# A hybrid encoder layer on one core: other blocks for two first product units, a norm's matmul six blocks later, plain passes in four groups

## The chip, the cores and the metric

The kernel runs on one core of one Trainium2 chip. The metric is device microseconds of the whole program. The engines are named as in the profile: PE (TensorE, matmuls), PEld (its weight loads), DVE (VectorE), ACT (ScalarE), POOL (GpSimd) and SP (SyncE, which here only issues DMAs).

## The reference

One encoder layer for 512 tokens of width 2048, in float32:

```python
h = rms_norm(x, norm_gains[l, 0])
# h @ w_in -> 11 blocks of 512 columns, shared by four mixers:
# stick-breaking attention, differential attention, a gated linear recurrence, a short gated conv
mixed = jnp.concatenate([y_sb, y_df, y_lru, y_sc], axis=-1) @ w_out[l]
x = x + rms_norm(mixed, norm_gains[l, 1])
h = rms_norm(x, norm_gains[l, 2])
u = causal_dwconv(h @ w_up, conv_w)          # 2048 -> 8192, conv of 3 taps
g, up = jnp.split(u, 2, axis=-1)
x = x + rms_norm((gelu(g) * up) @ w_down, norm_gains[l, 3])   # 4096 -> 2048
```

The change lies in the second half: the norm before the feed-forward part, the up projection and the down projection.

## The kernel before, in words

Activations are kept transposed, features on the 128 partitions and tokens along the free axis. Every float32 operand is split into a high part `hi` (rounded to the type that PE multiplies in) and a low part `lo` (the rest). A product is the sum of three passes: weight hi by activation hi, weight hi by activation lo, weight lo by activation hi. Splitting is a copy on ACT (`w_hi`, L99 and L1048; `a`, L189) and a subtraction on DVE (`w_lo`, L100 and L1049; L190).

**Groups.** `group` (from L125) makes four output blocks of 128 features from 8 chunks of weights. A chunk is 512 KB, loaded by SP into one of three `w_raw` buffers, then split into one of three `w_hi` and three `w_lo` buffers. With `both`, the tokens of one half (256) have their hi and lo side by side in memory, and the two passes with weight hi are joined into one matmul of 512 columns (hi into the left half of a PSUM bank, lo into the right), followed by one of 256 columns for weight lo. The two halves of the bank then have to be added: `sum_of` copies the left half on ACT (L952) and adds the right on DVE (L953). Without `both` all three passes have 256 columns and go into one place, and a copy suffices.

**Order of the work.** PE runs its instructions in the order in which the program is written. Work beside the matmuls is hung on a clock of blocks: `tick` counts four blocks a chunk, and `at(block, fn)` runs `fn` when the clock gets there. The other engines' instructions are put in order ahead of time by a scheduler that goes by priorities: what stands under `high_priority` (weight loads and splits, taking results out of PSUM) goes first. Each engine, and each DMA queue, then runs its list strictly in that order.

**The second norm.** The out projection's last two column groups are done for the first 256 tokens, then for the last 256. After each of the two halves `residual` (L842) normalises, adds x, and hangs the squares of the new x (L868 on ACT, summed by L870 on DVE), the scaled copies (L876) and `norm2` on the clock. `norm2` (L880) sums the squares over partitions with a matmul by ones on PE (L885), works out the reciprocal root (L200 to L206) and makes the operands of the up projection (L891, L189, L190). After the second half `sums_of_h` (L904) also makes the sums of operands T1, T3 and T4 (L911 to L918).

**Plain up units.** `up_plain` (L1002) does the first four of 32 blocks of gate and of value as four ordinary groups: gate and value for the first tokens, then gate and value for the last.

**Product units.** The rest of the up projection, and most of the down projection, run as `seven` (L1063): a 2 by 2 block product with seven products in place of eight. A unit loads the four weight blocks a11, a12, a21, a22 and makes the sums s1 = a21 + a22, s2 = a11 + s1, s3 = a11 + a21 and s4 = a12 + s2, each sum by a DVE add (L1054) or by an accumulating DMA from POOL's queue (L1058, from s3's own copy of a11). The products come in the order 11 (a11), 21 (a12), T2 (s2), T1 (s1), T3 (s3), 22 (s4), T4 (a22); L1079 are its passes with weight hi, L1084 those with weight lo. T2 and T3 go into the PSUM bank that 11 used, so each must wait until `take` has read it (ACT L1143, DVE L1144 to L1146 in the up units, DVE L1247 in the down units).

Blocks of weights lie in `w_raw` buffers or in `spare`, a tile that takes over the place of an operand that is done with: in the up units the second `mg` tile (free after the splits of `split_t2` and of T4, L190), in the down units `act`'s tile `a0` (free when PE has read the last plain down group). The first unit of each kind (`first`) finds these places still in use. `ystage` and `gst` are two small pools of 512 KB buffers (`ys`), through which the down projection's operands are loaded.

Of the kernel before, what the change touches and what calls it, by code (L numbers as in the profile page):

```python
# [9 lines left out]
F32 = mybir.dt.float32  # L10
# [38 lines left out]
def trunk(ctx: ExitStack, tc: tile.TileContext, xT, params, consts, wgate, w_in, w_out, w_up0, w_up, w_dn, w_dns, out):  # L49
# [734 lines left out]
    with ExitStack() as ph:  # L784
# [57 lines left out]
        def residual(hf):  # L842

            ts = HALVES[hf]
            ss1[hf].rstd(rstd1[:, ts])
            acc = ph2.tile([P, 2, S // 2], F32, name="s2")
            for q in range(4):
                for i in range(2):
                    m = mg[q][hf][:, 2 * i:2 * i + 2]
                    V.tensor_tensor(out=m, in0=m, in1=repeated(rstd1[:, ts], 2), op=ALU.mult)  # L850
                if q < 2:
                    G.dma_start(out=xs[q][hf], in_=mg[q][hf], accum_op=ALU.add)
            for q in range(2, 4):
                for i in range(2):
                    m, x = (t[q][hf][:, 2 * i:2 * i + 2] for t in (mg, xs))
                    V.tensor_tensor(out=x, in0=x, in1=m, op=ALU.add)
            for n, q in enumerate((0, 2, 1, 3)):
                at(clock[0] + 19 + 4 * n // 3, lambda n=n, q=q: squares(hf, q, acc, n == 0))
                at(clock[0] + 25 + 2 * n, lambda q=q: scaled(hf, q))
            at(clock[0] + 37, lambda: norm2(hf, acc))  # L860

        def squares(hf, q, acc, first):

# [138 lines left out]
        def up_plain(half, ts):  # L1002
            def evac(u, ps):
                if ts.start == 0:
                    ub[half, u] = up_tile()
                t = ub[half, u]
                sum_of(t[:, 2 + ts.start:2 + ts.stop], ps)
                return (lambda: done(u)) if ts.stop == S else None

            def done(u):  # L1010
                if half == 0:
                    gates[u] = conv(ub[half, u], half, u)
                else:
                    later.append(lambda: glu(u, gates[u], conv(ub[half, u], half, u)))
            group([w_up0[half, c] for c in range(8)], act_h, act_l, natural, evac,
                  mm_tile if half == 0 else pa_tile, ts, both=act_b)

        for half in range(2):
            up_plain(half, H0)
# [17 lines left out]
        def by4(t):  # L1037
            return flat(t).rearrange("p (a b) -> p a b", a=4)
# [24 lines left out]
        def seven(src, tops, take, first=False, place=None):  # L1063
# [23 lines left out]
            if place is None:  # L1087
                a11, a21 = raw(spare[n], src[0, 0]), raw(spare[2 + n], src[1, 0])
                a12, s3, a22 = (w_raw() for _ in range(3))
            else:  # L1090
                a11, a12, a21 = (w_raw() for _ in range(3))
                s3, a22 = place
                raw(a11, src[0, 0])
                raw(a21, src[1, 0])
            if first:
                raw(a22, src[1, 1])
                if place is None:
                    add(s3, a11, a21)
                add(a21, a21, a22)
            else:  # L1100
                dma_add(a21, by4(src[1, 1]))
            if place is not None or not first:
                raw(s3, src[0, 0])
                dma_add(s3, by4(src[1, 0]))
            s1 = a21
            raw(a12, src[0, 1])
            o11 = operand(a11)
            add(a11, a11, s1)
            s2 = a11
# [26 lines left out]
        def up_unit(unit):  # L1136
# [9 lines left out]
                    taken.append(V.tensor_tensor(out=t, in0=t, in1=ps[:, 256:512], op=ALU.add))  # L1146

            taken = []
            steps = seven(w_up[unit - 4], tops, take, first=unit == 4)
            next(steps)  # L1150
            gate = conv(u[0], 0, unit)
            if later:
# [88 lines left out]
        def down_unit(n):  # L1241
# [4 lines left out]
                    for part in (ps[:, 0:256], ps[:, 256:512]):  # L1246
                        V.tensor_tensor(out=t, in0=t, in1=part, op=ALU.subtract if i else ALU.add)  # L1247

            place = (spare[0], by4(gst.tile([P, 2, S], F32, name="ys"))) if n == 0 else None
            for _ in seven(w_dns[n], dtops, take, n == 0, place):  # L1250
                pass

# [168 lines left out]
```

## Time and profile before

| | |
|---|---|
| runs of the kernel before | 1786.59, 1786.46 and 1779.22 us, median 1786.46 |
| the profiled execution | 1781.3 us, of which its span is 1779.6 |
| PE busy | 1728.9 us, 97% of the span |
| PE weight loads busy | 1472.4 us, 83% |
| DVE busy | 1259.5 us, 71% |
| ACT busy | 903.0 us, 51% |
| POOL busy | 161.1 us, 9% |

Busy is the union of an engine's instructions. The ends of matmuls are modelled, so the pace of PE is read from the starts of matmuls that follow each other and not from their durations.

### The profile page before, as it was taken

Reading aid. Unit: us, or ns where it says so; the run is one execution under the profiler, and the core shown is the slowest. Engines: PE = TensorE matmul, PEld = TensorE weight load, DVE = VectorE, ACT = ScalarE, POOL = GpSimd, SP = SyncE. Lnnn points to the kernel's source line nnn. Section 1 sums busy time; section 2 is a strip of 40 time slices with the busy share of each in tenths; the row PEclk is TensorE's granted clock in tenths of the full one; section 3 lists DMA queues with packets and bytes.
Section 4 is the critical chain, followed back from the end, with each engine's and each line's share of the span. In section 5 each row is a group of like instructions: output and inputs, shape, how many; then the busy total and the mean of one; then the engine's idle time right before and its main releaser. Section 6 shows DMA issues by size and latency. Waiting matters only on the chain. (4 is left out here: it accounts for less than half of the span.)

```text
span 1779.6 us, 23837 instructions
## 1 busy us (share of the span) xinstructions
PE 1728.9 (97%) x8896; PEld 1472.4 (83%) x8896; DVE 1259.5 (71%) x1943; ACT 903.0 (51%) x1351; POOL 161.1 (9%) x228
## 2 busy tenths in 40 slices
PE   8999999999999999999999999999999999999995
PEld 7778788887888888788788888888888878888884
DVE  7885576566656424889898888788888886775337
ACT  6443576665334335776555555555555663333342
POOL 0000011100000011100011111111111001110120
PEclk9999999999999999999999999999999999999998
DMA  7234222242222625775788888888888668878233
GB/s 254 81 103 144 83 78 78 77 154 80 92 95 89 201 96 188 224 237 166 206 225 244 238 227 223 235 232 218 239 229 229 194 195 215 224 196 287 95 114 135
DMA packets 97020, 308.06 MB, mean 173 GB/s; under 512 B 10468, under 2 KB 14820, under 8 KB 96904
## 3 DMA queue, kind: packets, MB, share of 16 engines
q1 hardware_dynamic: 80056, 247.29, 41.2%
q0 software_dynamic: 15696, 57.15, 17.1%
q10 hardware_dynamic: 1152, 2.10, 0.3%
q8 instruction: 70, 1.15, 0.3%
q14 instruction: 46, 0.38, 0.1%
HBM read 265.59 MB, written 21.24 MB: 161 GB/s over the span
## 5 line engine op out<-in xcount | busy, mean ns | idle before, releaser
L100 DVE TENSOR_TENSOR w_lo<-w_raw,w_hi 128x1024 fp32r<-128x1024 f32 (+1 forms) x207 | 253.2, 1224 | 248.1 <-PE mm L157 140.4
L99 ACT CAST w_hi<-w_raw 128x1024 fp32r<-128x1024 f32 (+1 forms) x207 | 216.4, 1045 | 307.2 <-PE mm L157 192.0
L157 PE MATMUL mm<-a,w_hi 128*128 128x512 f32 x1280 | 310.1, 392 | 2.1 <-DVE t L330 2.1
L1079 PE MATMUL mm<-a,w_hi 128*128 128x512 f32 x1088 | 275.9, 396 | 8.4 <-DVE m L1247 5.3
L157 PEld LDWEIGHTS mm<-a,w_hi 128*128 128x128 f32 x1280 | 238.7, 188 | 52.4 <-DVE t L330 2.6
L1048 ACT CAST w_hi<-w_raw 128x1024 fp32r<-128x1024 f32 x145 | 152.0, 1049 | 202.1 <-PE mm L1079 164.5
L1079 PEld LDWEIGHTS mm<-a,w_hi 128*128 128x128 f32 x1088 | 197.6, 191 | 44.9 <-issue 5.7
L1049 DVE TENSOR_TENSOR w_lo<-w_raw,w_hi 128x1024 fp32r<-128x1024 f32 x145 | 177.0, 1221 | 37.6 <-ACT w_hi L1048 37.4
L157 PE MATMUL mm<-a,w_lo 128*128 128x512 f32 x640 | 166.2, 397 | 0.0
L1084 PEld LDWEIGHTS mm<-a,w_lo 128*128 128x128 f32 x1088 | 148.6, 191 | 12.0 <-DVE w_lo L1049 1.3
L1084 PE MATMUL mm<-a,w_lo 128*128 128x256 f32 x1088 | 151.8, 282 | 0.9 <-DVE w_lo L1049 0.9
L1079 PE MATMUL mm<-xs,w_hi 128*128 128x512 f32 x576 | 144.3, 392 | 0.2 <-DVE ub L1146 0.2
L157 PEld LDWEIGHTS mm<-a,w_lo 128*128 128x128 f32 x640 | 117.8, 189 | 24.1 <-issue 1.5
L1048 ACT CAST w_hi<-mg 128x1024 fp32r<-128x1024 f32 x84 | 87.6, 1044 | 81.1 <-PE mm L1079 81.1
L1079 PEld LDWEIGHTS mm<-xs,w_hi 128*128 128x128 f32 x576 | 103.7, 189 | 18.9 <-DVE ub L1146 0.4
L1049 DVE TENSOR_TENSOR w_lo<-mg,w_hi 128x1024 fp32r<-128x1024 f32 x84 | 102.4, 1220 | 19.9 <-ACT w_hi L1048 19.9
L1079 PE MATMUL mm<-mg,w_hi 128*128 128x512 f32 x352 | 88.3, 393 | 1.4 <-DVE m L1247 1.4
L1084 PEld LDWEIGHTS mm<-xs,w_lo 128*128 128x128 f32 x576 | 78.6, 190 | 5.6
L1146 DVE TENSOR_TENSOR ub<-ub,mm 128x256 f32<-128x256 f32 x196 | 81.2, 414 | 0.0
L1084 PE MATMUL mm<-xs,w_lo 128*128 128x256 f32 x576 | 80.3, 282 | 0.0
L1079 PEld LDWEIGHTS mm<-mg,w_hi 128*128 128x128 f32 x352 | 63.3, 189 | 13.0 <-ACT xs L189 1.6
L1247 DVE TENSOR_TENSOR m<-m,mm 128x256 f32<-128x256 f32 x112 | 46.5, 416 | 36.5 <-PE mm L1084 36.3
(308 smaller groups left out, 2725.1 us busy)
## 6 DMA issues: line engine op xcount, KB each, us to landing
w_raw<-in_w_up_dram SPq DMA_DIRECT2D x115, 512.0 KB, 5.7
w_raw<-in_w_in_dram SPq DMA_DIRECT2D x87, 512.0 KB, 3.3
mg<-in_w_up_dram SPq DMA_DIRECT2D x56, 512.0 KB, 4.2
w_raw<-in_w_out_dram SPq DMA_DIRECT2D x48, 512.0 KB, 3.3
w_raw<-in_w_dn_dram SPq DMA_DIRECT2D x38, 512.0 KB, 3.3
w_raw<-mg POOLq DMA_DIRECT2D x28, 512.0 KB, 6.2
mg<-in_w_up_dram POOLq DMA_DIRECT2D x27, 512.0 KB, 7.8
w_raw<-in_w_up_dram POOLq DMA_DIRECT2D x27, 512.0 KB, 8.8
```

The lines of the kernel that those rows point to most:

```text
L99: w_split.append(A.copy(out=hi[:, sl], in_=raw[:, sl]))
L100: V.tensor_tensor(out=lo[:, sl], in0=raw[:, sl], in1=hi[:, sl].bitcast(F32), op=ALU.subtract)
L157: T.matmul(pss[u], lhsT=a, rhs=b, start=c == 0 and kk == 0 and not low and i == 0, stop=False)
L1048: w_split.append(A.copy(out=by4(hi), in_=v))
L1049: V.tensor_tensor(out=by4(lo), in0=v, in1=by4(hi).bitcast(F32), op=ALU.subtract)
L1079: T.matmul(ps.rearrange("p (a t) -> p a t", a=2), lhsT=hi[:, k * P:(k + 1) * P], rhs=tops[name][k], start=first and k == 0, stop=False, **kw)
L1084: T.matmul(ps[:, 0:256], lhsT=lo[:, k * P:(k + 1) * P], rhs=tops[name][k][:, 0], start=False, stop=k == 7, **kw)
L1146: taken.append(V.tensor_tensor(out=t, in0=t, in1=ps[:, 256:512], op=ALU.add))
L1247: V.tensor_tensor(out=t, in0=t, in1=part, op=ALU.subtract if i else ALU.add)
```

## The change

Three edits stand in one diff.

```diff
-            at(clock[0] + 37, lambda: norm2(hf, acc))
+            at(clock[0] + 43, lambda: norm2(hf, acc))
...
-                sum_of(t[:, 2 + ts.start:2 + ts.stop], ps)
+                A.copy(out=t[:, 2 + ts.start:2 + ts.stop], in_=ps)
...
             group([w_up0[half, c] for c in range(8)], act_h, act_l, natural, evac,
-                  mm_tile if half == 0 else pa_tile, ts, both=act_b)
+                  mm_tile if half == 0 else pa_tile, ts)
...
                 a11, a12, a21 = (w_raw() for _ in range(3))
                 s3, a22 = place
                 raw(a11, src[0, 0])
+                raw(a12, src[0, 1])
                 raw(a21, src[1, 0])
             if first:
                 raw(a22, src[1, 1])
-                if place is None:
-                    add(s3, a11, a21)
                 add(a21, a21, a22)
             else:
                 dma_add(a21, by4(src[1, 1]))
-            if place is not None or not first:
-                raw(s3, src[0, 0])
-                dma_add(s3, by4(src[1, 0]))
+            raw(s3, src[0, 0])
+            dma_add(s3, by4(src[1, 0]))
             s1 = a21
-            raw(a12, src[0, 1])
+            if place is None:
+                raw(a12, src[0, 1])
...
-            steps = seven(w_up[unit - 4], tops, take, first=unit == 4)
+            place = (spare[0], spare[2]) if unit == 4 else None
+            steps = seven(w_up[unit - 4], tops, take, unit == 4, place)
...
-            place = (spare[0], by4(gst.tile([P, 2, S], F32, name="ys"))) if n == 0 else None
+            place = [by4(t.tile([P, 2, S], F32, name="ys")) for t in (ystage, gst)] if n == 0 else None
```

The second norm's matmul moves by six blocks on the clock, a chunk and a half. On PE, at the first of its two places (the out projection's last group, `pa<-a`, two rows for one chunk and two of its operands), it moves behind the passes with weight lo of one chunk and all passes of the next:

```order
 L149 MATMUL pa<-a_82,w_lo 128x256 x8
 L149 MATMUL pa<-a_80,w_hi 128x512 x8
-L885 MATMUL mm<-s_5766,con 128x256 x2
 L149 MATMUL pa<-a_80,w_lo 128x256 x8
 L149 MATMUL pa<-a_80,w_hi 128x512 x8
 L149 MATMUL pa<-a_80,w_lo 128x256 x8
+L885 MATMUL mm<-s_5766,con 128x256 x2
 L149 MATMUL pa<-a_81,w_hi 128x512 x8
```

Between the old and the new place now stand 24 matmuls.

The first up unit (unit 4) takes a11, a12 and a21 into `w_raw` buffers and leaves s3 and a22 to the shared place `mg`. SP's queue before, from the last chunk of the plain up units (L98) on; `w_raw_7168` is a22, the four `mg` are a11 and a21 of units 4 and 5, `w_raw_7166` is a12:

```order
L98 DMA w_raw_7122<-in_w_up0_dram 128x1024
L1042 DMA w_raw_7168<-in_w_up_dram 128x1024
L1042 DMA mg_7156<-in_w_up_dram 128x1024 x4
L1042 DMA w_raw_7166<-in_w_up_dram 128x1024
L1042 DMA mg_7156<-in_w_up_dram 128x1024
```

And of the change; `w_raw_7404`, `7405` and `7406` are a11, a12 and a21, the first two `mg` are s3's copy of a11 and a22, the next two are unit 5's a11 and a21:

```order
L98 DMA w_raw_7358<-in_w_up0_dram 128x1024
L1042 DMA w_raw_7404<-in_w_up_dram 128x1024
L1042 DMA w_raw_7405<-in_w_up_dram 128x1024
L1042 DMA mg_7396<-in_w_up_dram 128x1024 x2
L1042 DMA w_raw_7406<-in_w_up_dram 128x1024
L1042 DMA mg_7396<-in_w_up_dram 128x1024 x2
```

The blocks of the first two products now stand ahead of every load that needs the shared place; a21 still stands behind two of them.

The first down unit takes s3 into `ystage` where it had the shared place `a0`. DVE before, from the last split of the down projection's operands (L190) on; the row with `a0` is the split of s3, L1247 are the takes:

```order
L190 TENSOR_TENSOR mg_12363<-ys_12520,mg_12363 128x512
L1247 TENSOR_TENSOR m30_12342<-m30_12342,mm_12735 128x256
L1049 TENSOR_TENSOR w_lo_12799<-w_raw_12740,w_hi_12798 128x1024
L1247 TENSOR_TENSOR m30_12342<-m30_12342,mm_12735 128x256
L1247 TENSOR_TENSOR m30_12342<-m30_12342,mm_12737 128x256 x2
L1049 TENSOR_TENSOR w_lo_12821<-a0_12733,w_hi_12820 128x1024
L1247 TENSOR_TENSOR m30_12342<-m30_12342,mm_12735 128x256
L1049 TENSOR_TENSOR w_lo_12843<-w_raw_12739,w_hi_12842 128x1024
L1247 TENSOR_TENSOR m30_12342<-m30_12342,mm_12735 128x256
```

And of the change; s3 is `ys_12975`:

```order
L190 TENSOR_TENSOR mg_12604<-ys_12761,mg_12604 128x512
L1247 TENSOR_TENSOR m30_12583<-m30_12583,mm_12977 128x256
L1049 TENSOR_TENSOR w_lo_13041<-w_raw_12982,w_hi_13040 128x1024
L1247 TENSOR_TENSOR m30_12583<-m30_12583,mm_12977 128x256
L1247 TENSOR_TENSOR m30_12583<-m30_12583,mm_12979 128x256
L1049 TENSOR_TENSOR w_lo_13063<-ys_12975,w_hi_13062 128x1024
L1247 TENSOR_TENSOR m30_12583<-m30_12583,mm_12979 128x256
L1247 TENSOR_TENSOR m30_12583<-m30_12583,mm_12977 128x256
```

The order on DVE is nearly the same; what differs is the place from which s3 is read.

## Rows read from the trace of the kernel before

**Rows 1.** The page's first part: engine, busy us, share of the span, instructions.

```profile
PE 1728.9 (97%) x8896; PEld 1472.4 (83%) x8896; DVE 1259.5 (71%) x1943; ACT 903.0 (51%) x1351; POOL 161.1 (9%) x228
```

**Rows 2.** Who waited for whom, PE: us in total, times, longest.

```profile
PE mm L885 <- DVE s L870: 7.5, 2, 4.0
```

**Rows 3.** Stretches: length, busy us of each engine, granted clock, DMA share.

```profile
740.00:750.00 10.00, 6.01 (x21) 4.84 (x21) 6.40 (x9) 7.67 (x16) 0.00 (x0) 0.66 0.51 165
...
744.00:863.00 119.00, 114.25 (x621) 99.64 (x622) 106.73 (x142) 83.03 (x132) 1.76 (x2) 0.95 0.59 195
...
804.50:857.60 53.10, 53.10 (x305) 46.68 (x304) 52.03 (x60) 37.05 (x47) 0.00 (x0) 1.00 0.51 168
```

**Rows 4.** Timeline of PE, first norm matmul: start, us, engine, line [idle before <-releaser].

```profile
738.32 2.11 PE L149 MATMUL pa<-a,w_hi 128*128 128x512 f32 x8
744.42 2.04 PE L885 MATMUL mm<-s,con 128*128 128x256 f32 x4 [3.98 <-DVE s L870]
745.90 2.27 PE L149 MATMUL pa<-a,w_lo 128*128 128x256 f32 x8
...
750.39 0.88 PE L149 MATMUL pa<-a,w_lo 128*128 128x256 f32 x6
```

**Rows 5.** Timeline of DVE at the same place.

```profile
740.19 3.48 DVE L100 TENSOR_TENSOR w_lo<-w_raw,w_hi 128x1024 fp32r<-128x1024 f32 x3
743.60 0.68 DVE L870 TENSOR_TENSOR s<-s,f 128x512 f32<-128x512 f32 x1
```

**Rows 6.** Timeline of PE, second norm matmul.

```profile
792.66 2.00 PE L149 MATMUL pa<-a,w_hi 128*128 128x512 f32 x8
798.15 2.04 PE L885 MATMUL mm<-s,con 128*128 128x256 f32 x4 [3.49 <-DVE s L870]
...
804.54 1.10 PE L149 MATMUL pa<-a,w_lo 128*128 128x256 f32 x8
```

**Rows 7.** Timeline of PE inside the first plain up group.

```profile
770.29 2.00 PE L149 MATMUL mm<-a,w_hi 128*128 128x512 f32 x8
772.13 1.12 PE L149 MATMUL mm<-a,w_lo 128*128 128x256 f32 x8
773.09 2.00 PE L149 MATMUL mm<-a,w_hi 128*128 128x512 f32 x8
```

**Rows 8.** Groups of DVE instructions, 750 to 862: shapes, count | busy, mean ns | idle.

```profile
L953 DVE TENSOR_TENSOR ub<-ub,mm 128x256 f32<-128x256 f32 x8 | 3.2, 416 | 0.4 <-ACT ub L952 0.4
```

**Rows 9.** Timeline of PE, start of the first up unit.

```profile
862.41 2.11 PE L1079 MATMUL mm<-a,w_hi 128*128 128x512 f32 x8 [0.83 <-ACT w_hi L1048]
...
868.81 3.62 PE L1079 MATMUL mm<-a,w_hi 128*128 128x512 f32 x8 [2.18 <-ACT w_hi L1048]
872.26 0.99 PE L1084 MATMUL mm<-a,w_lo 128*128 128x256 f32 x7
```

**Rows 10.** Timeline of all engines ahead of it (SPq is SP's queue).

```profile
855.27 2.35 DVE L190 TENSOR_TENSOR mg<-mg 128x1024 fp32r<-128x1024 f32 x2
...
857.65 1.75 SPq L1042 DMA_DIRECT2D mg<-in_w_up_dram  x4
...
859.44 0.75 SPq L1042 DMA_DIRECT2D w_raw<-in_w_up_dram  x1
```

**Rows 11.** Timeline of PE, first down unit.

```profile
1467.40 2.06 PE L1079 MATMUL mm<-a,w_hi 128*128 128x512 f32 x8 [2.38 <-DVE m L1247]
...
1472.09 1.11 PE L1084 MATMUL mm<-a,w_lo 128*128 128x256 f32 x8
1476.17 3.65 PE L1079 MATMUL mm<-a,w_hi 128*128 128x512 f32 x8 [2.96 <-DVE m L1247]
1479.64 1.14 PE L1084 MATMUL mm<-a,w_lo 128*128 128x256 f32 x8
```

**Rows 12.** Timeline of DVE in the first down unit.

```profile
1457.82 1.22 DVE L1054 TENSOR_TENSOR w_raw<-w_raw,ys 128x1024 f32<-128x1024 f32 x1 [1.06 <-DMA ys<-in_w_dns_dram]
...
1473.00 1.22 DVE L1049 TENSOR_TENSOR w_lo<-a,w_hi 128x1024 fp32r<-128x1024 f32 x1 [4.77 <-ACT w_hi L1048]
```

## Prediction

> **What bounds the kernel now.** I read the engines' shares first: PE is busy 97% of the span, DVE 71% [rows 1]. So PE is the engine whose idle time counts, and the question is where in the second half it waits. The view of who waited for whom has the norm matmul (L885) first: 7.5 us in two waits for the summed squares [rows 2]. The timelines then give each place, and the stretches tell what the clock does after a wait.
>
> Four places matter. At each I take as lost the time between what the matmuls would have needed at full pace and when the next ones started. That pace is read where PE is fed: eight matmuls of 512 columns start over 1.84 us (0.230 each), eight of 256 over 0.96 (0.120 each) [rows 7].
>
> *First norm matmul.* Eight wide matmuls start at 738.32 and would be done by 740.16. L885 starts at 744.42, waiting for DVE's last sum [rows 4]. The granted clock over 740 to 750 is 0.66, so half of full pace (1.2 of 2.4 GHz) for a part of it [rows 3]: L885's four matmuls take 1.48 us until 745.90, I count 0.74 at full pace. Then 0.96 and 1.84 should lead to 743.70; the next narrow pass starts at 750.39 [rows 4]. Lost: 6.7 us.
>
> *Second norm matmul.* In the same way 792.66 + 1.84 + 0.74 + 2.80 = 798.04, against 804.54 [rows 6]. Lost: 6.5.
>
> *First up unit.* 0.83 before the first pass; from 862.41 on, two wide passes and a narrow one need 4.64 us, which leads to 867.05, and the next narrow one starts at 872.26 [rows 9]. Lost: 5.2 + 0.8 = 6.0. The cause stands in the queue: SP holds its four loads into `mg` until DVE's split ends at 857.6, and the load of a12, needed for the second product, stands behind them (859.44) [rows 10].
>
> *First down unit.* A wait of 2.38 ahead of T2 and one of 2.96 ahead of T3 [rows 11]. The second is a queue on DVE: the split of s3 waits 4.77 us for its cast, which waits for s3 itself, and the takes that free the bank for T3 stand behind it [rows 12]. From 1472.09 a narrow pass and a wide one should end at 1474.89; the next narrow pass starts at 1479.64 [rows 11]. Lost: 4.75.
>
> **The change, part by part.**
>
> *The norm's matmul, six blocks later.* A chunk and a half of matmuls that needs nothing from the norm comes ahead of it: 0.96 + 1.84 + 0.96 = 3.76 us at the first place (in the second, plain group 0.96 + 1.92 + 0.96). At the first place these need w_lo, and the first of DVE's three splits ends at about 741.4 (740.19 and a third of 3.48, rounded up) [rows 5], so PE waits 1.2 us there; the norm comes at 740.16 + 1.2 + 3.76 = 745.1, after the last sum (743.60 + 0.68 = 744.3) [rows 5]. Gain 6.7 − 1.2 = 5.5. At the second place PE gets to the norm at 794.50 + 3.84 = 798.3, in the old times; before, the sum released it at 798.15 [rows 6]. No wait, gain 6.5. What is late next: the operands for the next group, which are made from the norm. The chain from rstd to them lies on DVE, beside four chunks of matmuls (4 × 2.80 = 11.2 us) where it had five and a half; at 98% DVE busy (52.03 of 53.10) in the stretch behind the second norm [rows 3] this is the thinnest cover in the change. I price it at 0.3 us for each half and keep 3 us each as the other end.
>
> *Plain passes.* For 64 pairs of operand and chunk in each of four groups, 0.230 + 0.120 becomes 3 × 0.120 [rows 7]: 0.010 × 256 = 2.6 us more on PE, all on the path. DVE loses 16 adds of 0.416 [rows 8], 6.7 us in a stretch where it is nearly full, which is what the splits need if PE is to run without its stalls. Stretches of 24 narrow matmuls do not occur before; those of eight keep 0.120 to their end, and I take that.
>
> The Trainium skill ("TensorE: Matmul & The Clock Gate", section Back-to-back issue gap) gives N/2.4 + 2.5 ns for a matmul alone at full clock, 109 and 216 ns; by it three narrow passes would cost 2.5 ns more than the joined pair, 0.6 us in all (an estimate from that page), and it adds that in a stream of weight loads and matmuls both set the pace. This case's rows have 120 and 230, so the trace is above the formula, and the rows decide.
>
> *First up unit.* a11 and a12 no longer wait for `mg`: both come with the buffers that the last plain chunks free. s3 and a22 go to `mg`, and a21 has to come behind them in SP's queue. With these in place T2 is the next that can be late: it needs a21 + a22, added to a11, cast. `mg` comes free when DVE has made the splits of T4 and T2. Counted in the order of the change, DVE has between the second norm and that 16 splits of weights and 16 steps of the operands of the same size (1.16 each, the pitch of the three [rows 5]) and 16 of half the size: 46 us, and it starts on them some 2.5 us after PE has passed the norm. PE has 20 plain chunks of 2.88 = 57.6 until the unit. So `mg` should be free 7 to 9 us ahead of the unit, where it was 4.8 ahead (857.6 to 862.4) [rows 9, 10]. The queue's five loads took until the a12 cast that released PE at 868.81, 9 us from its issue [rows 9, 10]; a21 now is the third. I forecast 0.5 us left of 6.0, gain 5.5; the ends are 0 and 6.0.
>
> *First down unit.* s3's load no longer waits for PE to be done with `a0`; in SP's new order it even stands ahead of a22's, which arrives at 1457.8 [rows 12]. Before, s3's load and its accumulating DMA were both done between there and the split at 1473.00 [rows 12], 15 us; now only the second is left after 1457.8, and it has until about 1471 for T3 to start on time. So DVE's list should no longer stop there: gain 4.75. The wait of 2.38 ahead of T2 comes from DVE's row of work behind a22's arrival, which the order leaves as it was: it stays.
>
> **Sum.** −5.5 − 6.5 + 0.6 + 2.6 − 5.5 − 4.75 = −19.0 us. The profiled execution took 1781.3, so 1762.3 for one like it. The median of the runs shown is 5.2 above that execution, the lowest run 2.1 below: I forecast **1764**.
>
> **Rivals.**
>
> *DVE takes it back.* DVE had 12.3 us idle between 744 and 863 (106.73 busy of 119) [rows 3], while PE stalled. If it keeps as much idle time and only loses the 6.7 us of adds, PE meets late splits or a late s2 in unit 4. Then the two norms, the plain passes and unit 4 together give at most 6.7 us; with the down unit 11.5, so 1770 against the profiled execution and 1772 on the forecast's scale. For it: 98% [rows 3]. Against it: in that stretch of 53 us PE had no wait, so a full DVE kept up with PE at full pace while it still had the adds to do.
>
> *The place does not help unit 4.* a21 is behind two loads that wait for `mg`, so if `mg` is not free sooner the wait moves from the second product to the third, and only the two norms and the down unit give: −13.5, 1768 against the profiled execution and near 1770 on the forecast's scale. For it: the new queue order. Against it: the earlier split order on DVE.
>
> *Narrow passes hold PE up.* The other side. If in a run of 24 the pace falls from 0.120 to what a weight load takes from start to end (PEld busy 1472.4 over 8896 is 0.166 each [rows 1]), 768 matmuls cost 35 us more: +16, 1797 as measured against the profiled execution. It decides from 0.145 on (19 us over 768) and is slower by over 0.5% from 0.157. Against it: eight in a row show no such drift [rows 7].
>
> **Chances.** Forecast, with 15 us or more gained: 0.62. DVE takes it back: 0.20, of which half are gains above 0.5% (8.9 us, about what a measurement of this kernel can tell from no change). Unit 4 not helped: 0.11, still faster. Narrow passes slow: 0.04. Something else that leaves no change: 0.03. So faster 0.83, same 0.13, slower 0.04. The range: down to 1756, where the down unit's T2 wait goes too, nothing new is left over, and the runs are as low as the lowest of before; up to 1775, where DVE's rival and the median's 5 us come together.
>
> **What would show it.** Right: L885 with no wait for L870 and the clock at 1.00 behind it; a plain chunk of 24 matmuls in 2.88 us; unit 4's first three passes at full pace; T3 in the first down unit without a wait, T2 still with one of about 2.4. Wrong: waits of PE for L190's operands at the start of a plain up group, for a weight's w_lo (L100) in them, or ahead of T2 in unit 4; starts of narrow matmuls further apart than 0.120.

## The result and the profile after

The changed kernel took 1772.14 us (median of 6 runs, 1768.99 to 1775.05) against 1786.53 for the kernel before (median of 6). The ratio is 0.9937, 95% interval 0.9922 to 0.9953: faster by 8 to 14 us. A second set of runs gave 0.9928 (0.9914 to 0.9942). The forecast was 1764. The medians shown differ by more than this ratio says (14.4 us, a ratio of 0.992); how the two fit together is open. The direction was right and the time lies in the range, but the 15 us or more to which the forecast gave 0.62 did not come.

The profiled execution took 1772.23 us, 9.1 less than that of before (1781.3), so what follows has to add up to 9.1, where the forecast's sum is 19.0. PE's busy share hardly moves; its busy time counts the plain passes and the slow stretches too. The first part of the page:

```profile
PE 1727.5 (98%) x9152; PEld 1484.7 (84%) x9152; DVE 1252.2 (71%) x1926; ACT 902.1 (51%) x1351; POOL 162.0 (9%) x229
```

The view of who waited for whom, PE from 737 to 920 (us in total, times, longest). The wait of L885 that led in [rows 2] is gone. In its place a product of an up unit (L1079) waits for a take (L1145), and there are four waits for the weights of a chunk (L99, L100):

```profile
PE mm L1079 <- DVE ub L1145: 5.9, 3, 4.7
PE pa L157 <- ACT w_hi L99: 1.3, 2, 0.8
PE pa L149 <- DVE w_lo L100: 1.0, 1, 1.0
PE pa L149 <- ACT w_hi L99: 0.3, 1, 0.3
```

The stretches, with the columns of [rows 3]. The granted clock is 1.00 through both norms, where it was 0.66 at the first; the only low one is at the first up unit. At 783 to 794 ACT is busy for the whole stretch and the DMA engines for 0.95 of it:

```profile
738.00:751.00 13.00, 11.67 (x66) 9.83 (x65) 10.04 (x10) 11.04 (x21) 2.65 (x3) 1.00 0.69 238
...
783.00:794.00 11.00, 9.69 (x79) 9.28 (x78) 9.15 (x12) 11.00 (x22) 0.00 (x0) 1.00 0.95 344
794.00:855.00 61.00, 61.00 (x508) 60.90 (x507) 57.91 (x64) 45.22 (x63) 0.00 (x0) 1.00 0.62 195
855.00:872.00 17.00, 12.34 (x60) 10.48 (x59) 11.98 (x19) 8.21 (x14) 2.98 (x4) 0.80 0.96 249
```

PE's timeline. The first norm answers to [rows 4]: L885 starts without a wait. What is lost there is 0.5 ahead of 739.42 and 1.3 ahead of 742.55, both for weights. Then a plain chunk, with sixteen and eight narrow matmuls, from 758.48 to 761.35. Then the two waits in the last plain group for the first tokens, 784.38 and 791.15. Then the first up unit, which answers to [rows 9]: the first two products run at full pace, and T2, due at 860.09 + 0.96 = 861.05, starts at 865.86. Its eight wide matmuls take 3.58 us until 869.44, where 1.84 is full pace; the granted clock of that stretch is 0.50, which is 1.2 GHz. Last the first down unit, which answers to [rows 11]: T2 at 1463.04, 1.9 late, and T3 at 1468.68 without a wait:

```profile
739.42 2.11 PE L149 MATMUL pa<-a,w_hi 128*128 128x512 f32 x8 [0.31 <-ACT w_hi L99]
742.55 1.22 PE L149 MATMUL pa<-a,w_lo 128*128 128x256 f32 x8 [1.02 <-DVE w_lo L100]
...
746.40 1.03 PE L885 MATMUL mm<-s,con 128*128 128x256 f32 x4
...
758.48 2.08 PE L157 MATMUL mm<-a,w_hi 128*128 128x256 f32 x16
...
761.35 0.88 PE L157 MATMUL mm<-a,w_hi 128*128 128x256 f32 x6
...
784.38 2.18 PE L157 MATMUL pa<-a,w_hi 128*128 128x256 f32 x16 [0.56 <-ACT w_hi L99]
...
791.15 1.10 PE L157 MATMUL pa<-a,w_hi 128*128 128x256 f32 x7 [0.75 <-ACT w_hi L99]
...
855.45 2.00 PE L1079 MATMUL mm<-a,w_hi 128*128 128x512 f32 x8
...
860.09 1.11 PE L1084 MATMUL mm<-a,w_lo 128*128 128x256 f32 x8
865.86 3.78 PE L1079 MATMUL mm<-a,w_hi 128*128 128x512 f32 x8 [4.66 <-DVE ub L1145]
869.44 0.78 PE L1084 MATMUL mm<-a,w_lo 128*128 128x256 f32 x3
...
1463.04 2.06 PE L1079 MATMUL mm<-a,w_hi 128*128 128x512 f32 x8 [1.74 <-DVE m L1247]
...
1468.68 2.00 PE L1079 MATMUL mm<-a,w_hi 128*128 128x512 f32 x8
```

What T2 of the up unit waited for, from the timelines of the other engines; it answers to [rows 10]. At 850.23 SP issues the two loads into the shared place `mg`, s3's copy of a11 and a22. a21 (`w_raw`) goes out at 852.03, because its buffer is that of the last plain chunk, which DVE has split only then. DVE's s1 = a21 + a22 starts at 858.98, when a21 has landed. s2 follows at 860.78, its cast at 862.03. On ACT the casts of s2 and s1 run one after the other and only then comes the copy that begins the first product's take (L1142, 863.93). On DVE its second half (L1145, 865.39) stands behind both splits:

```profile
850.23 0.80 SPq L1042 DMA_DIRECT2D mg<-in_w_up_dram  x2
...
852.03 0.33 SPq L1042 DMA_DIRECT2D w_raw<-in_w_up_dram  x1
...
858.98 1.23 DVE L1054 TENSOR_TENSOR w_raw<-w_raw,mg 128x1024 f32<-128x1024 f32 x1 [1.39 <-DMA w_raw<-in_w_up_dram]
...
860.78 1.22 DVE L1054 TENSOR_TENSOR w_raw<-w_raw 128x1024 f32<-128x1024 f32 x1
...
862.03 1.99 ACT L1048 CAST w_hi<-w_raw 128x1024 fp32r<-128x1024 f32 x2 [0.51 <-DVE w_raw L1054]
...
863.11 2.36 DVE L1049 TENSOR_TENSOR w_lo<-w_raw,w_hi 128x1024 fp32r<-128x1024 f32 x2 [0.41 <-ACT w_hi L1048]
863.93 0.37 ACT L1142 COPY ub<-mm 128x256 f32<-128x256 f32 x1
...
865.39 0.41 DVE L1145 TENSOR_TENSOR ub<-ub,mm 128x256 f32<-128x256 f32 x1
```

So a first reading: the wait of unit 4 did not go. It moved from the second product to the third and has two parts, a late load and a take that stands far back in two queues. The experiments were made to test this, and to give each edit its share.

### The profile page after: what moved, and what is told of

Read it like the earlier page. It is cut to its first block, busy times and chain, and to the rows that moved or that the text cites. A ratio compares the mean times of both kernels' runs of the same rounds, so it can differ in the third digit from the quotient of the medians.

```text
span 1770.5 us, 24333 instructions
## 1 busy us (share of the span) xinstructions
PE 1727.5 (98%) x9152; PEld 1484.7 (84%) x9152; DVE 1252.2 (71%) x1926; ACT 902.1 (51%) x1351; POOL 162.0 (9%) x229
## 4 chain that ended last, share of the span: by engine, by line
PE 89%; DVE 5%; DMA 3%; ACT 2%; issue 1%; POOLq 0%; POOL 0%; SPq 0%; DVEq 0%; ACTq 0%
PE mm L157 33%; PE mm L1079 24%; PE mm L1084 12%; PE pa L157 4%; PE pa L149 3%; PE mm L149 2%; PE mm L121 2%; PE mm L123 2%; PE mm L122 2%; PE pa L587 1%; DVE w_lo L100 1%; DMA w_raw<-in_w_up_dram 1%; DVE w_lo L1049 1%; PE pa L692 1%; DVE m L1298 0%
## 5 line engine op out<-in xcount | busy, mean ns | idle before, releaser
L100 DVE TENSOR_TENSOR w_lo<-w_raw,w_hi 128x1024 fp32r<-128x1024 f32 (+1 forms) x207 | 253.6, 1226 | 251.2 <-PE mm L157 141.1
L99 ACT CAST w_hi<-w_raw 128x1024 fp32r<-128x1024 f32 (+1 forms) x207 | 216.2, 1045 | 292.1 <-PE mm L157 195.1
L157 PE MATMUL mm<-a,w_hi 128*128 128x512 f32 (+1 forms) x1504 | 339.9, 377 | 2.1 <-DVE t L330 2.1
L157 PEld LDWEIGHTS mm<-a,w_hi 128*128 128x128 f32 x1504 | 267.1, 189 | 52.2 <-DVE t L330 2.6
L1079 PE MATMUL mm<-a,w_hi 128*128 128x512 f32 x1088 | 274.6, 395 | 6.8 <-DVE ub L1145 5.0
L1079 PEld LDWEIGHTS mm<-a,w_hi 128*128 128x128 f32 x1088 | 197.0, 190 | 42.4 <-DVE ub L1145 5.4
L157 PE MATMUL mm<-a,w_lo 128*128 128x512 f32 (+1 forms) x752 | 182.1, 380 | 0.0
L1084 PEld LDWEIGHTS mm<-a,w_lo 128*128 128x128 f32 x1088 | 148.9, 191 | 10.7
L157 PEld LDWEIGHTS mm<-a,w_lo 128*128 128x128 f32 x752 | 132.5, 190 | 24.0 <-issue 1.5
L1079 PE MATMUL mm<-xs,w_hi 128*128 128x512 f32 x576 | 144.5, 393 | 1.0 <-DVE ub L1145 1.0
L1079 PEld LDWEIGHTS mm<-xs,w_hi 128*128 128x128 f32 x576 | 103.8, 189 | 19.9 <-DVE ub L1145 1.4
L1079 PE MATMUL mm<-mg,w_hi 128*128 128x512 f32 x352 | 88.3, 393 | 1.5 <-DVE m L1247 1.5
L1145 DVE TENSOR_TENSOR ub<-ub,mm 128x256 f32<-128x256 f32 x196 | 81.6, 416 | 0.0
L1079 PEld LDWEIGHTS mm<-mg,w_hi 128*128 128x128 f32 x352 | 63.4, 189 | 13.1 <-issue 1.9
L1247 DVE TENSOR_TENSOR m<-m,mm 128x256 f32<-128x256 f32 x112 | 46.7, 418 | 36.4 <-PE mm L1084 36.3
```

What stands on the lines that cost most here:

```text
L99: w_split.append(A.copy(out=hi[:, sl], in_=raw[:, sl]))
L100: V.tensor_tensor(out=lo[:, sl], in0=raw[:, sl], in1=hi[:, sl].bitcast(F32), op=ALU.subtract)
L157: T.matmul(pss[u], lhsT=a, rhs=b, start=c == 0 and kk == 0 and not low and i == 0, stop=False)
L1079: T.matmul(ps.rearrange("p (a t) -> p a t", a=2), lhsT=hi[:, k * P:(k + 1) * P], rhs=tops[name][k], start=first and k == 0, stop=False, **kw)
L1084: T.matmul(ps[:, 0:256], lhsT=lo[:, k * P:(k + 1) * P], rhs=tops[name][k][:, 0], start=False, stop=k == 7, **kw)
```

## Experiments

All ratios are to the kernel before on the same chip, with their 95% intervals; 0.001 is 1.8 us.

| kernel | ratio | interval |
|---|---|---|
| the change (two sets) | 0.9937, 0.9928 | 0.9922 to 0.9953, 0.9914 to 0.9942 |
| before + norm's matmul later | 1.0000 | 0.9991 to 1.0008 |
| before + plain passes | 0.9986 | 0.9976 to 0.9996 |
| before + places of up unit 4 | 1.0007 | 0.9999 to 1.0016 |
| before + places of the first down unit | 0.9958 | 0.9945 to 0.9971 |
| change − norm's matmul later | 0.9940 | 0.9927 to 0.9953 |
| change − plain passes | 0.9962 | 0.9949 to 0.9975 |
| change − places of up unit 4 | 0.9923 | 0.9908 to 0.9938 |
| change, a21 and s3 exchanged (two sets) | 0.9907, 0.9901 | 0.9893 to 0.9921, 0.9884 to 0.9917 |
| change, T1 ahead of T2 | 0.9934 | 0.9922 to 0.9946 |
| change without 4.9 us of DVE's work | 0.9928 | 0.9917 to 0.9940 |
| change, squares later | 0.9920 | 0.9908 to 0.9932 |
| exchanged + squares later | 0.9919 | 0.9904 to 0.9933 |
| exchanged + gates' convolutions later | 0.9950 | 0.9933 to 0.9967 |
| the last + squares later | 0.9932 | 0.9917 to 0.9947 |
| change without the first take | 0.9930 | 0.9914 to 0.9946 |
| exchanged without the first take | 0.9907 | 0.9891 to 0.9924 |

**Each part alone.** First the norm's matmul:

```diff
-            at(clock[0] + 37, lambda: norm2(hf, acc))
+            at(clock[0] + 43, lambda: norm2(hf, acc))
```

> The kernel before with the norm's matmul six blocks later and nothing else. Theory (the norm's edit holds by itself; what is missing was lost at the first up unit and in two new waits near 783-791): about -9 us, made of -4.6 at the first place, -6.4 at the second and up to +2 in waits for w_hi and w_lo while the residual's DMAs run. Rival (DVE takes it back, and the plain passes are needed for the gain): with the sixteen adds still on DVE, PE meets late splits in the plain groups and at unit 4, and no more than -5 us are left.

Alone this edit gave nothing: 0.0 us, −1.6 to +1.4. The rival came nearer than the theory. At the second place PE is done with the passes ahead of L885 at 791.83 + 0.96 = 792.8 and then waits, since the sum comes only 0.9 us earlier than in [rows 6]. And the shared place comes free at 854.52, 3.1 us earlier than in [rows 10], while PE reaches unit 4 at 856.5, 4.9 us earlier than before. There it waits for what it had won. PE's and SP's timelines:

```profile
791.83 1.11 PE L149 MATMUL pa<-a,w_lo 128*128 128x256 f32 x8
797.25 1.19 PE L885 MATMUL mm<-s,con 128*128 128x256 f32 x2 [4.32 <-DVE s L870]
...
854.52 1.76 SPq L1042 DMA_DIRECT2D mg<-in_w_up_dram  x4
...
860.04 3.52 PE L1079 MATMUL mm<-a,w_hi 128*128 128x512 f32 x8 [3.34 <-ACT w_hi L1048]
```

The plain passes:

```diff
-                sum_of(t[:, 2 + ts.start:2 + ts.stop], ps)
+                A.copy(out=t[:, 2 + ts.start:2 + ts.stop], in_=ps)
...
-                  mm_tile if half == 0 else pa_tile, ts, both=act_b)
+                  mm_tile if half == 0 else pa_tile, ts)
```

> The kernel before with three narrow passes in the plain up groups and nothing else. Theory (the passes cost 2.7 us on PE, and DVE frees the shared place some us earlier): between -1 and +2 us, the price less what unit 4's wait for a12 shrinks. Rival (the narrow passes hold PE up): +10 us or more, seen as chunks longer than 2.9 us.

2.5 us faster (0.7 to 4.3), a little more than the theory gave. What I had not seen: this edit alone takes away the whole wait at the second norm, at the old place. Without the adds DVE's last sum ends at 795.2, 2.8 us earlier than in [rows 6] (PE's release there, 798.0), and PE comes there 1.9 us later than 792.66 + 1.84; 1.65 of that it is already late at the first norm (746.07 against 744.42). The four matmuls of L885 follow PE's passes without a wait:

```profile
794.46 2.08 PE L157 MATMUL pa<-a,w_hi 128*128 128x256 f32 x16
796.38 1.03 PE L885 MATMUL mm<-s,con 128*128 128x256 f32 x4
```

The third edit's first half, with the order of loads that goes with it:

```diff
+            place = (spare[0], spare[2]) if unit == 4 else None
+            steps = seven(w_up[unit - 4], tops, take, unit == 4, place)
```

> The kernel before with the new places in up unit 4 and nothing else (with the order of loads that goes with them, in the first down unit too). Theory (the wait moves from the second product to the third): within 1.5 us of before, and PE waits some 4 to 6 us ahead of T2. Rival (the place helps, and in the changed kernel it is only DVE's lateness that undoes it): -4 us or more.

1.2 us slower (−0.2 to +2.9), as the theory had it. The first two products run at full pace, then T2 waits, and then T3:

```profile
869.72 2.11 PE L1079 MATMUL mm<-a,w_hi 128*128 128x512 f32 x8 [2.54 <-ACT w_hi L1048]
...
878.57 1.84 PE L1079 MATMUL mm<-xs,w_hi 128*128 128x512 f32 x4 [2.99 <-DVE ub L1145]
```

Its second half:

```diff
+            place = [by4(t.tile([P, 2, S], F32, name="ys")) for t in (ystage, gst)] if n == 0 else None
```

> The kernel before with the new places in the first down unit and nothing else. Theory (independent of the rest): -5 us, T3 without a wait, and the wait ahead of T2 some 0.5 us shorter. Rival (half of the down unit's gain is an effect of the rest of the change): less than -3 us.

7.5 us faster (5.2 to 9.8), somewhat more than expected: this part alone, with the a12 load that moves up in the queue with it, is some two thirds of what the whole change gave. In its trace T2 and T3 wait 0.4 and 0.5 us, where [rows 11] have 2.38 and 2.96; this is T2:

```profile
1465.59 2.08 PE L1079 MATMUL mm<-a,w_hi 128*128 128x512 f32 x8 [0.38 <-DVE m L1249]
```

The two waits belong together. In the kernels with the old place in the down unit T2 waits 2.4, 1.0, 0.0 and 1.4 us (before, norm later, plain passes, places of unit 4) and T3 3.0, 5.0, 5.9 and 4.5: what T2 does not wait, T3 does, 5.3 to 6.0 us in all.

**The change less one part.** The same lines, turned round.

```diff
-            at(clock[0] + 43, lambda: norm2(hf, acc))
+            at(clock[0] + 37, lambda: norm2(hf, acc))
```

> The changed kernel with the norm's matmul back at its old place; the rest as changed. Theory (the plain passes alone already take away the second norm's wait, so the six blocks give only the first place's 4.6 us, and the waits near 783 to 791 and unit 4 take part of that back): 1 to 4 us slower than the changed kernel. Rival (both places count, as in the forecast's sum): 9 us or more slower.

0.9940, which is 0.5 to 2 us slower than the change's two sets and inside their intervals. PE's waits: L885 waits at the first place alone, the waits for weights near 784 to 791 are not there, and T2 of unit 4 waits 3.3 in place of 4.7:

```profile
PE mm L885 <- DVE s L870: 4.0, 1, 4.0
PE mm L1079 <- DVE ub L1145: 3.3, 1, 3.3
```

So of the norm's edit only the first place counts, and what it wins there (4.9 us) is lost again: 1.7 at 784 to 791, and at unit 4 1.4 of wait and 1.6 of low clock (T2's wide matmuls take 1.95 us here, 3.58 in the change).

```diff
-                A.copy(out=t[:, 2 + ts.start:2 + ts.stop], in_=ps)
+                sum_of(t[:, 2 + ts.start:2 + ts.stop], ps)
...
-                  mm_tile if half == 0 else pa_tile, ts)
+                  mm_tile if half == 0 else pa_tile, ts, both=act_b)
```

> The changed kernel with the joined passes and the two-part sum back in the plain up groups; norm, up unit and down unit as changed. Theory (the plain passes pay for themselves: their 2.7 us on PE buy DVE's 16 adds, and the norm's six blocks need that): 2 to 4 us slower than the changed kernel, with a wait of 3 us or more at the second L885. Rival (the passes are only a price, as in the forecast's sum): 2.7 us faster than the changed kernel.

0.9962: 4.5 to 6 us slower than the change. The theory held, at more than its size, and the wait at the second L885 is 4.8 us in spite of the later place:

```profile
PE mm L885 <- DVE s L870: 4.8, 1, 4.8
```

```diff
-            place = (spare[0], spare[2]) if unit == 4 else None
+            place = None
```

> The changed kernel with the old places in up unit 4; the rest as changed. Theory (the new place only moves the wait, as it did alone, where it cost 1.2 us): within 2 us of the changed kernel, with the wait ahead of the second product back. Rival (the place gives its gain once DVE is relieved): 4 us or more slower than the changed kernel.

0.9923, 1 to 2.5 us faster than the change and inside the intervals of its two sets. The edit from which I forecast 5.5 us gave nothing, alone and in company. The waits are back at the first and the second product, 1.01 and 1.77 us, and the second product's wide matmuls take 3.00.

**Why T2 waits in unit 4.** First the order of the queue: a21 in `mg`, s3 in the third buffer.

```diff
-                a11, a12, a21 = (w_raw() for _ in range(3))
-                s3, a22 = place
+                a11, a12, s3 = (w_raw() for _ in range(3))
+                a21, a22 = place
```

> The changed kernel with a21 and s3 in each other's place in up unit 4: a21 and a22 in the shared place, whose two loads are the first in the queue when it comes free, s3 in the third w_raw buffer. Theory (T2 waits because a21 stands behind the two loads that wait for the shared place): s1 can be added some 2 us earlier, the wait ahead of T2 falls from 4.9 to 2.5 us or less and the slow clock behind it goes or halves: -3 to -5 us against the changed kernel. Rival (the shared place comes free too late whatever the order): the wait stays at 4 us or more, time within 1 us of the changed kernel.

> The kernel with a21 and s3 in each other's place, again: ratio to the kernel before 0.989 to 0.992 if the exchange is worth what its first run showed; 0.993 or more if that was chance.

0.9907 and 0.9901, about 5 us faster than the change by the means of the two sets. It is the fastest kernel here. s1 can now be added at 857.45 with the unit's start at 856.42; in the changed kernel that was 858.98 with the start at 855.45, 2.5 us later against PE. T2's wait falls to 2.3 (2.9 in the second set), and its wide matmuls take 1.98 us in place of 3.58:

```profile
857.45 1.22 DVE L1054 TENSOR_TENSOR mg<-mg 128x1024 f32<-128x1024 f32 x1 [0.78 <-DMA mg<-in_w_up_dram]
...
864.45 2.14 PE L1079 MATMUL mm<-a,w_hi 128*128 128x512 f32 x8 [2.29 <-DVE ub L1147]
866.43 1.10 PE L1084 MATMUL mm<-a,w_lo 128*128 128x256 f32 x8
```

Then the other part, the take. In the changed kernel and in the exchanged one the first product's take is left out:

```diff
-            take(0, lo_, x, True)
+            if not first or dn:
+                take(0, lo_, x, True)
...
-            take(0, lo_, w, False)
+            take(0, lo_, w, first and not dn)
```

> The changed kernel without the take of the first product in up unit 4 (its result is left out of the sums; the second product's take then starts them), so that T2's bank is free as soon as that product ends. Theory (T2's wait has two parts: until s2 is cast, and then until the take, which stands behind the casts of s2 and s1 on ACT and both splits on DVE): T2 waits 2.0 to 2.5 us in place of 4.7, and for ACT's cast (L1048). Rival (all of the wait is the late load, the take would be in time with an earlier one): 4 us or more.

> The same left out of the kernel with a21 and s3 in each other's place. Theory (the exchange removed the part that is the load's, what is left is the take's): T2 waits under 0.6 us. Rival (the loads are still late): 1.5 us or more.

Both as the theory had it. With the late load, T2 waits 2.25 us and for ACT's cast:

```profile
865.02 2.11 PE L1079 MATMUL mm<-a,w_hi 128*128 128x512 f32 x8 [2.25 <-ACT w_hi L1048]
```

With the early load it does not wait at all. But T3 then does, for the take of T2, so the times are no better (0.9930 and 0.9907):

```profile
861.04 2.12 PE L1079 MATMUL mm<-a,w_hi 128*128 128x512 f32 x8
...
869.34 3.69 PE L1079 MATMUL mm<-xs,w_hi 128*128 128x512 f32 x8 [2.44 <-DVE ub L1148]
```

In the first kernel T3 waits likewise, 3.48 us. So by these traces T2's 4.7 us are some 2.3 for the load and 2.4 for the place of the take. Between the repeats of the change and of the exchange (4.99 and 2.94) the load's part is 2.1. The take was only left out; a kernel with the take ahead of the casts was not run. In the change's trace there is room for it: the first product is done at 858.25, and ACT stands idle for the 3.2 us up to 860.90.

Another order of products:

```diff
+            if t1_first:
+                product(y, o1, "T1", True)
+                take(1, hi_, y, True)
             product(x, o2, "T2", False)
```

> The changed kernel with T1 ahead of T2 in up unit 4, so that the third product needs s1 and a free bank and not s2 and the take of the first product. Theory (T2 waits for s2, its cast, and the take that stands behind two casts on ACT and two splits on DVE): the wait ahead of the third product falls to 1.5 us or less, T2 after it waits under 1 us: -3 to -5 us against the changed kernel. Rival (the loads themselves are late): 3 us or more of wait stay, only moved to T1.

0.9934, no better. The third product still waits 2.73 us, and T3, which now follows T2 in the same bank, waits 4.06. Theory and rival each had a part of it: the load is late, and a product that follows another in one bank pays for the take between them.

```profile
861.34 2.11 PE L1079 MATMUL mm<-xs,w_hi 128*128 128x512 f32 x8 [2.73 <-ACT w_hi L1048]
...
871.25 1.22 PE L1079 MATMUL mm<-xs,w_hi 128*128 128x512 f32 x2 [4.06 <-DVE ub L1149]
```

Is it the amount of DVE's work?

```diff
-            for i in range(2):
-                t1, h21, h22 = mg[i][0], mg[2 + i][0], mg[2 + i][1]
-                V.scalar_tensor_tensor(out=h22, in0=t1, scalar=-1.0, in1=h22, op0=ALU.mult, op1=ALU.subtract)
-                V.scalar_tensor_tensor(out=h21, in0=h22, scalar=-1.0, in1=h21, op0=ALU.mult, op1=ALU.subtract)
```

> The changed kernel without the four combinations that make the operands of T4 and T2 (L917, L918; 4 x 1.23 = 4.9 us of DVE); these products then multiply other numbers, at the same cost. Theory (DVE's full row of work decides when the shared place comes free, so my count of its work was what failed): the place is free some 4 to 5 us earlier against PE's clock, T2 in unit 4 waits 2 us or less: -3 to -6 us against the changed kernel. Rival (the order of the queue alone): T2 still waits over 3.5 us.

0.9928, as the second set of the change. T2 waits 3.40 us, between the 2 of the theory and the 3.5 of the rival. The theory's first step fell here. With 4.9 us less to do, DVE leaves the shared place free at 849.35, 5.6 us ahead of the unit's start (854.96), where it was 5.2. In the order of its list other work, convolution taps (L976 here; this kernel's line numbers are four lower), moved ahead of the last split (L190), which kept its place against PE:

```profile
845.63 1.42 DVE L976 SCALAR_TENSOR_TENSOR f<-ub,par,f 128x512 f32<-128x512 f32 x2
846.96 1.23 DVE L100 TENSOR_TENSOR w_lo<-w_raw,w_hi 128x1024 fp32r<-128x1024 f32 x1
848.09 1.23 DVE L190 TENSOR_TENSOR a<-mg,a 128x1024 fp32r<-128x1024 f32 x1
...
849.35 0.80 SPq L1038 DMA_DIRECT2D mg<-in_w_up_dram  x2
...
864.11 3.13 PE L1075 MATMUL mm<-a,w_hi 128*128 128x512 f32 x8 [3.40 <-DVE ub L1141]
```

And the rest of DVE's work between the load and the take:

```diff
-                if half == 0:
-                    gates[u] = conv(ub[half, u], half, u)
-                else:
-                    later.append(lambda: glu(u, gates[u], conv(ub[half, u], half, u)))
+                if half == 1:
+                    later.append(lambda: glu(u, conv(ub[0, u], 0, u), conv(ub[1, u], 1, u)))
```

> a21 and s3 in each other's place, and the convolutions of the four plain gates taken out of the stretch ahead of up unit 4 and done one by one in the later units, as the values' already are. Theory (what is left of T2's wait, 2.6 us, is the row of eight taps of 0.7 us and of casts that DVE and ACT have between the last plain chunk and the take): T2's wait falls below 1.3 us, about -1.5 us against the kernel with the two places exchanged alone. Rival (the loads' landing alone sets it): the wait stays at 2 us or more.

0.9950, 8 us slower than without it, and T2's wait is 3.07. The rival is nearer, but the load is not all of it. DVE now has idle time (4.39 us of it ahead of s1, for the load), and the take (L1145) still stands behind two splits; s2 was cast by 861.62, T2 starts after 863.90:

```profile
861.62 1.23 DVE L1047 TENSOR_TENSOR w_lo<-w_raw,w_hi 128x1024 fp32r<-128x1024 f32 x1 [1.11 <-ACT w_hi L1046]
862.76 1.22 DVE L1047 TENSOR_TENSOR w_lo<-mg,w_hi 128x1024 fp32r<-128x1024 f32 x1
863.90 0.42 DVE L1145 TENSOR_TENSOR ub<-ub,mm 128x256 f32<-128x256 f32 x1
```

Most of the 8 us is lost in unit 4 itself. T3 waits 3.65 us and its wide matmuls take 3.20: on ACT the take of T2 stands behind a cast that waits 6.1 us for the accumulating DMA of s4. From the start of the unit to the start of its sixth product it is 24.3 us, in the exchanged kernel's repeat 18.6.

**The two new waits near 784 and 791.**

```diff
-                at(clock[0] + 19 + 4 * n // 3, lambda n=n, q=q: squares(hf, q, acc, n == 0))
-                at(clock[0] + 25 + 2 * n, lambda q=q: scaled(hf, q))
+                at(clock[0] + 22 + 4 * n // 3, lambda n=n, q=q: squares(hf, q, acc, n == 0))
+                at(clock[0] + 28 + 2 * n, lambda q=q: scaled(hf, q))
```

> The changed kernel with the squares and the scaled copies of the second norm three blocks later on the clock (22 and 28 for 19 and 25), the norm's matmul where it was. Theory (the waits for w_hi and w_lo near 783 to 791 come from ACT standing at a square that waits 6.5 us for the residual's accumulating DMA, with the casts of weights behind it): these waits, 1.8 us, go, and the norm's matmul still finds its sum: -1 to -2 us. Rival (the DMAs are simply full there, at 0.95 of their time): the waits stay within 0.5 us of 1.8, since the weights land late, or L885 waits again.

0.9920, 1.4 to 3 us better than the change's two sets, but inside the interval of one of them. The view of waits has one of the two waits left, 0.6 us in place of 1.3. In the changed kernel ACT stands 6.5 us at the first square, which waits for the residual's accumulating DMA, and the cast for the chunk comes behind it and two more instructions:

```profile
781.84 0.63 ACT L868 ACTIVATE s<-xs 128x512 f32<-128x512 f32 x1 [6.53 <-DMA xs<-mg]
...
783.30 1.03 ACT L99 CAST w_hi<-w_raw 128x1024 fp32r<-128x1024 f32 x1
```

With the later squares ACT still stands there for 6.0 us, so the edit moved the casts ahead but not the stall. And at the first norm's place PE waits 2.15 us for `w_hi` where it waited 0.31 in the change and 0.86 in its repeat; it comes there 2.6 us earlier than in the change, a lead that it had before the edited part. All waits for weights together are 3.2 us, against 2.6 and 3.3 in the two executions of the change. So the traces don't show that these waits went; how much of them is the DMA engines' 0.95 is open.

> The changed kernel with a21 and s3 in each other's place and with the second norm's squares and scaled copies three blocks later. Theory (two stalls apart from each other): -5.4 us from the first and -1 to -3 us from the second, ratio to the kernel before 0.988 to 0.990. Rival (what PE gains in the norm it waits for in unit 4): 0.9905 or more.

> As the last, and with the second norm's squares and scaled copies three blocks later. Theory (the two stalls are apart, and each edit takes its own): 2 to 3 us below the kernel without the later squares, some 9 to 10 us below the changed kernel, ratio to the kernel before about 0.988. Rival (what PE gains there it loses at up unit 4, since the shared place does not come free earlier): within 1 us of the kernel without the later squares.

> The changed kernel again, as the yardstick for the two others on the same chip: ratio to the kernel before within 0.992 to 0.995, by either theory.

These two have the diffs above together. With a21 and s3 exchanged, the later squares no longer help (0.9919 against 0.9907 and 0.9901), as the rival had it. With the gates' convolutions later too they give 3 us (0.9932 against 0.9950), as the theory had it, though the two intervals overlap, but from a level that is 8 us worse, so that neither comes near the 0.988 or 0.990 of the theories. The change itself repeated as expected.

## Why the prediction held in part, and where it failed

By its own steps, in us of the profiled execution:

| step | forecast | measured |
|---|---|---|
| first norm matmul | −5.5 | −4.9 (1.8 of 6.7 left) |
| second norm matmul | −6.5 | −6.5 |
| operands late | +0.6 | 0; instead +1.7 at 784 and 791 |
| plain passes | +2.6 | +2.6 (2.87 for a chunk) |
| first up unit | −5.5 | +0.5 (4.8 of wait and 1.7 at the low clock, 6.0 before) |
| first down unit | −4.75 | −4.8 at T3, −0.6 at T2 |
| up unit 5 | none | +1.8 in this execution, none in the repeat's |
| sum | −19.0 | −10.2, against −9.1 between the two executions |

Of the 1.1 between these two sums 0.8 lies ahead of all edits: the same two matmuls of L149 start at 666.66, at 665.84 before. Another 0.25 is the narrow pass behind T2 of unit 4, 1.21 us (869.44 to 870.65) for 0.96.

**The step that failed is the first up unit.** I wrote that `mg` should be free 7 to 9 us ahead of the unit, and forecast "0.5 us left of 6.0". Three things were wrong in it.

- The place came free 5.2 us ahead, not 7 to 9. I had counted DVE's work against PE's time. The run without 4.9 us of that work shows that the amount is not what sets it: the last split keeps its place in DVE's list, just ahead of the last plain chunk's, and other work fills the time.
- I took a21 as third in a queue of loads that all start with the shared place. It has a buffer of its own to wait for, and goes out 1.8 us after the others. Giving it the shared place instead took 2.4 us off T2's wait (2.1 between the repeats).
- I costed T2's operand as "added to a11, cast" and gave this no time. From a21's landing to T2 it is 6.9 us: two sums, a tap between them, a cast, and then the take of the first product behind two casts and two splits. A take behind a split gave the first down unit its T3 wait in [rows 12]; I read it there and didn't look for it in the unit that I was moving. The runs without the take show it: 2.4 us of the 4.7.

So it was the rival "The place does not help unit 4" that came, to which I gave 0.11, for the reason that it names. Of its 13.5 us, 1.7 went to the new waits, 0.5 to unit 4 and 1.8 to unit 5, which leaves 9.5; the other steps add 0.7.

**Where the sum was right for a wrong reason.** The second norm's 6.5 us came, but not through the norm's edit: the plain passes take that wait away by themselves, and with the joined passes the later place does not. The forecast had the two as separate terms, a gain and a price. In truth the price buys the gain, and the norm's edit has only the first place. What it wins there PE waits for later, so alone it is worth 0.0 us, and within the change 0.5 to 2, inside the intervals.

**What held.** The plain passes cost what the starts of matmuls said. The Trainium skill ("TensorE: Matmul & The Clock Gate", section Back-to-back issue gap) has a formula for a matmul alone at full clock by which they would cost 0.6 us in all (an estimate from that page); this trace does not agree, with 2.87 for a chunk of narrow passes against 2.80 in [rows 7], which over 32 chunks is 2.2 to 2.6. The first down unit's wait at T3 went as forecast. That the wait at T2 "stays" was wrong: it falls to 0.4 with this part alone, to 1.7 in the change and to nothing in the change's repeat, where T3 waits 0.6. The two waits share 5.3 to 6.0 us without the new place, and 0.6 to 1.7 are left with it in these three traces, which goes with the 7.5 us (5.2 to 9.8) that this part gave when timed alone. Why the rest is 0.6 in one execution of the change and 1.7 in another is open. The rival "DVE takes it back" was right about DVE, which is busy 57.91 of 61.00 us after the second norm, but wrong in its mechanism, as the run with less work shows.

## What to carry to other kernels

A wait that goes is a gain only if nothing later is fixed in time: ask for each microsecond won which release comes next, and whether that release moves with the engine that won it. When a load is moved to another buffer, list for every operand of the unit both the buffer's release and the place in the queue, and follow the chain from landing to the matmul instruction by instruction, takes of the bank included. Two edits that touch one wait should be tried alone and together before each is given its own term.

## What was not expected of the hardware

A wait can cost more than its length, and its length alone does not tell how much. After 4.66 us of idle time PE ran the eight wide matmuls of T2 in 3.58 us, at a granted clock of 0.50; after 2.29 us in the exchanged kernel the same eight took 1.98. But after 2.53 us in the exchanged kernel with later squares they took 3.38 (granted clock 0.54), and after 3.34 us in the change with the norm's matmul at its old place 1.95 (1.00). What decides it these runs don't show. At the first norm of the changed kernel, with two waits of 0.31 and 1.02, the clock stayed at 1.00. The load of a21 took 7 us from issue to use, with four other loads of 512 KB issued between 850.2 and 853.5 and the DMA engines at 0.94 of their time in these 7 us.
